# Weight halves, deferred transposes and background modulation in a hybrid diffusion layer

## The chip, the cores and the metric

The kernel runs on one core of a Trainium2 chip. The metric is device time in microseconds for one execution; where several executions were timed, the median is given. TensorE multiplies, VectorE and ScalarE do elementwise work, GpSimd does some sums and memsets and issues some DMAs, and the sync engine issues most DMAs. Each of these takes its own instructions in a fixed order.

## What is computed

One layer of a diffusion backbone, in float32, for 256 latent tokens and 256 context tokens of width 2048:

```python
mod_x = split(silu(c) @ w_mod + b_mod, 6)           # shift1, scale1, gate1, shift2, scale2, gate2
mod_c = split(silu(c_ctx) @ w_mod + b_mod, 6)
h  = rms_norm(x, g_mix) * (1 + mod_x[1]) + mod_x[0]   # the same for ctx with mod_c
qa, ka, va, qb, kb, vb, rb, lrf, lrb, gate_a, gate_b = split(h @ w_in)
o_attn = windowed_attention(qa, ka, va, context keys and values, sink)
o_gla  = bidirectional_gated_linear_attention(qb, kb, vb, decays from lrf, lrb)
y = (sigmoid(gate_a) * (o_attn @ w_attn_o)
     + sigmoid(gate_b) * ((rms_norm(o_gla) * silu(rb)) @ w_gla_o)) @ w_out
x = x + mod_x[2] * y
u = depthwise_conv3((rms_norm(x, g_ffn) * (1 + mod_x[4]) + mod_x[3]) @ w_up)
out = x + mod_x[5] * ((silu(u[:, :5632]) * u[:, 5632:]) @ w_down)
```

The weights are some 400 MB of float32, and each is used once.

## The kernel before

**Products in halves.** A float32 operand is split into a high half `hi` (rounded to the matmul type by ScalarE, line 61) and a low half `lo = x - hi` (VectorE, line 62). A product is three matmuls: hi·hi, hi·lo and lo·hi. `wload` (137) loads a chunk of 256 rows by 512 columns, 512 KB, into a ring of four buffers `raw`, on the sync engine's queue; `wsplit` (143) makes its halves `whi` and `wlo` in rings of three buffers each, at high priority.

**Projections.** `proj_nat` (152) computes tokens by features. Per chunk and per tile of 128 tokens it runs, for each of the two row tiles, activation-high by weight-high, activation-high by weight-low, activation-low by weight-high (163 to 165): 12 matmuls of 512 columns a chunk for two token tiles, 24 for four. `proj_T` (169) computes features by tokens, the weights stationary and 256 tokens moving: 24 matmuls a chunk (186 to 189), 48 when the context is taken along. Both accumulate in the four PSUM banks of the pool `acc`; at the end `evac` empties them.

**Ticks.** Before each chunk, `tick` (124) hands out work that runs beside the projections: `beside`, a generator with a pace (gated linear attention, or attention), and `bg_steps`, a list of steps with the pace `bg_rate`.

**Background modulation.** shift1 and scale1 are needed first, for both token kinds, and are computed on TensorE by `mod_both`. The other four parts, for the latent tokens alone, are done by `mod_latent` (225): for each part and each of four groups of 512 columns, eight steps, each of which loads 256 rows with `wload`, into the same `raw` ring and on the same queue as the weights, and adds them to `macc` with two VectorE instructions of 512 elements (line 239). After the last step of a group come a 32x32 transpose, a reduction, a tiny matmul on TensorE (247) and copies into the column tiles.

**Stages.** The order of the program is: shift1 and scale1 with the first projections (to about 220 us), gated linear attention for four heads beside the projections of its keys and values (to about 485), attention keys and values (to about 600), four query blocks with the attention of the block before beside them (to about 800), the GLA output gate, the merge of both branches and the output projection (to about 1300), and the ConvFFN in two halves, each with up-projections and then down-projections. The pace of the background is 0.7 steps a chunk in the first of these with background, then 2.0 for keys and values, 0 beside the attention, 0.5 until the output projection, where what remains is done at once.

**Transposes.** Attention keys (`ka_evac`, 676) and queries (`qa_block`, 689) are normalised and rotated by `norm_rope` on VectorE and ScalarE and transposed on TensorE in the evacuation itself. So are the gated GLA output and the merged branches (`to_T`, 776), and the residual stream (`wo_evac`, 838).

A scheduler orders each engine's instructions when the program is built, by priority and by what it expects to be ready; on the chip each engine then keeps that order. `W2(tag, ...)` takes a tile from a ring whose number of buffers stands in `F2_BUFS`; `bank` takes a PSUM bank, one for `main`, three for `side`.

Of the kernel before, what the change touches and what calls it, by code (L numbers as in the profile page):

```python
# [16 lines left out]
P = 128  # L17
# [13 lines left out]
def layer_kernel(ctx, tc, A, out):  # L31
# [6 lines left out]
    wr = pool(name="wr", bufs=4)  # L38
    wh = pool(name="wh", bufs=3)
# [8 lines left out]
    F2_BUFS = {"fa": 4, "fb": 4, "fc": 6, "mod": 2}  # L48
# [17 lines left out]
    def load(dst, src):  # L66
        """a load by the sync engine; while chain is open, issued in the order of the program"""
# [34 lines left out]
    def columns(name, parts, eng=G):  # L102
        rows = W2("mod", "rows", [P, P])
# [18 lines left out]
    beside = []  # L122

    def tick():
        """the steps of `beside`, a generator and its pace, and of the list"""
# [26 lines left out]
    def proj_nat(w, r0, c0, kts, lhs, evac):  # L152
        """out[token, feature] for 512 features; lhs[tile](kt) -> (hi, lo) [K, 128]"""
        banks = [acc.tile([P, 512], F32, name="acc", tag="acc") for _ in lhs]
        for k0 in kts[::2]:
# [3 lines left out]
            for i, l in enumerate(lhs):  # L159
                for k in range(nk):  # L160
                    kt = k0 + k
                    ahi, alo = l(kt)
                    PE.matmul(banks[i], ahi, hi[:, k, :], start=(kt == kts[0]), stop=False)  # L163
                    PE.matmul(banks[i], ahi, lo[:, k, :], start=False, stop=False)  # L164
                    PE.matmul(banks[i], alo, hi[:, k, :], start=False, stop=(kt == kts[-1]))  # L165
# [3 lines left out]
    def proj_T(w, c0, kts, rhs, evac):  # L169
        """out[feature, token] for 512 features; rhs: list of f(kt) -> (hi, lo) [K, 256]"""  # L170
# [3 lines left out]
        for k0 in kts[::2]:  # L174
# [3 lines left out]
            for f in range(4):  # L178
                for k in range(nk):
                    kt = k0 + k  # L180
                    whi, wlo = (x[:, k, f * P:(f + 1) * P] for x in (hi, lo))
                    for i, r in enumerate(rhs):
                        b = (f % per) if n == 1 else i
                        o = banks[f // per][:, b * T:(b + 1) * T]
                        ahi, alo = r(kt)
                        PE.matmul(o, whi, ahi, start=(kt == kts[0] and b == 0), stop=False,  # L186
                                  skip_group_check=True)
                        PE.matmul(o, whi, alo, start=False, stop=False, skip_group_check=True)  # L188
                        PE.matmul(o, wlo, ahi, start=False, stop=(kt == kts[-1]), skip_group_check=True)  # L189
# [6 lines left out]
    def mod_both(part, t0, n, dst):  # L196
        """steps for c and c_ctx on the tensor engine; dst[p, c, kt] for kt = t0..t0+n-1"""
# [27 lines left out]
    def mod_latent(part, j, dst):  # L225
        """steps for c alone: products summed over the row tiles on the vector engine"""
        a = []
        c0 = part * D + j * 512

        def step(k0):  # L230
            if k0 == 0:
                a.append(W2("mod", "macc", [P, 512]))
            raw = wload(w_mod[k0 * P:k0 * P + 256, c0:c0 + 512])
            for k in range(2):
                kt = k0 + k
                if kt == 0:
                    V.tensor_scalar(a[0], raw[:, 0, :], ccol[:, 0:1], None, op0=ALU.mult)
                else:
                    V.scalar_tensor_tensor(a[0], raw[:, k, :], ccol[:, kt:kt + 1], a[0],  # L239
                                           op0=ALU.mult, op1=ALU.add)  # L240
            if k0 == KT - 2:
                tr = W2("mod", "mtr", [P, 16, 32])
                V.transpose(tr.rearrange("p a c -> p (a c)"), a[0])
                rs = sm.tile([P, 16], F32, name="mrs", tag="mrs", bufs=2)
                V.tensor_reduce(rs, tr, op=ALU.add, axis=AX.X)
                pc = bank("pcl", (32, 16))
                PE.matmul(pc, sel[:, 0:32], rs, start=True, stop=True)
                pv = pc.rearrange("p (a b) -> p b a", b=4)
                d = dst[:, 4 * j:4 * j + 4]
                for b4 in range(4):  # L250
                    V.tensor_copy(d[32 * b4:32 * b4 + 32, :], pv[:, b4, :])
                b0 = part * 16 + j * 4
                V.tensor_tensor(d, d, bmod[:, b0:b0 + 4], op=ALU.add)

        return [lambda k0=k0: step(k0) for k0 in range(0, KT, 2)]
# [20 lines left out]
    def rms_scale(ss, n, shape):  # L276
        """(ss / n + eps) ** -0.5: exp(-ln / 2) with a Newton step"""
# [12 lines left out]
    def token_rows(tag, name, cols):  # L290
        """one factor a token, [P, 1] per tile of tokens, as a row in every partition"""
# [666 lines left out]
```

## Time and profile before

| what | value |
|---|---|
| runs | 2060.81, 2062.3 and 2058.01 us; median 2060.81 |
| profiled execution | span 2061.8 us from its first instruction to its last |
| mean granted TensorE clock | 0.990 of full speed |
| DMA | 413.71 MB, mean 201 GB/s |
| transfers on the sync queue | 406.89 MB |
| transfers on the GpSimd queue | 4.74 MB |

The page's chain of waits puts 60% of the span on TensorE, 11% on DMA, 8% on VectorE and 2% on ScalarE, with 18% of time in which an engine waited for nothing that the profile shows. In a row of a group, the numbers after the bar are the busy time, the mean duration of one instruction in ns, and the idle time of the engine just before the group's instructions with what ended it. A matmul's duration includes the depth of the pipeline, so that matmuls overlap, and their pace is read from counts in a stretch. A row of a stretch has its bounds, its length, and for each engine the busy time and the number of instructions, in the order TensorE, its weight loads, VectorE, ScalarE, GpSimd, and then the granted clock, the DMA share and GB/s. A row of waits has who waited for whom, the sum in us, how many times, and the longest.

### The profile page before, as it was taken

How to read it: one execution, taken by the hardware profiler on the slowest of the kernel's cores; microseconds unless marked ns; L12 is line 12 of the kernel's file. 1: busy time of each engine (PE TensorE's matmuls, PEld its weight loads, DVE VectorE, ACT ScalarE, POOL GpSimd, SP SyncE). 2: the span in 40 equal slices, each digit the busy share in tenths (PEclk: the TensorE clock that was granted, in tenths of full speed). 3: DMA queues.
4: the chain of work that ended last, by engine and by line, in shares of the span. 5: the costliest groups of instructions: out<-in, count | busy, mean ns of one | idle time of the engine just before them, and what ended most of it. 6: DMA issues, size and time to landing. Idle time of an engine off the chain costs nothing.

```text
span 2061.8 us, 30115 instructions
## 1 busy us (share of the span) xinstructions
PE 1999.2 (97%) x11792; PEld 1721.8 (84%) x11792; DVE 1405.7 (68%) x2149; ACT 937.4 (45%) x1306; POOL 41.9 (2%) x62
## 2 busy tenths in 40 slices
PE   6899999999999999999999999899999999999999
PEld 4679888888787777777787788899999889999987
DVE  4666778978867888777767665666666555666654
ACT  3323464552346665443334344554455334445533
POOL 0001100001000000000000000000000000000000
PEclk8999999999999999999999999999999999999999
DMA  9976434347664466787888875566666566666664
GB/s 347 337 247 197 120 111 123 113 118 226 213 186 114 121 194 192 254 270 260 264 279 272 294 235 184 164 184 184 184 183 184 194 193 187 184 184 183 183 209 150
DMA packets 214350, 413.71 MB, mean 201 GB/s; under 512 B 12548, under 2 KB 21092, under 8 KB 213184
## 3 DMA queue, kind: packets, MB, share of 16 engines
q1 hardware_dynamic: 212320, 406.89, 63.3%
q0 software_dynamic: 1360, 4.74, 0.8%
q8 instruction: 92, 1.51, 0.3%
q14 instruction: 50, 0.41, 0.1%
q10 hardware_dynamic: 528, 0.17, 0.0%
HBM read 409.63 MB, written 2.11 MB: 200 GB/s over the span
## 4 chain that ended last, share of the span: by engine, by line
PE 60%; issue 18%; DMA 11%; DVE 8%; ACT 2%; POOL 0%; DVEq 0%; ACTq 0%; POOLq 0%
PE acc L189 10%; PE acc L186 10%; PE acc L188 10%; PE acc L165 8%; PE acc L164 8%; PE acc L163 8%; DMA raw<-in_w_mod 8%; DVE wlo L62 3%; DVE macc L239 2%; DMA raw<-in_w_in 2%; PE pm L210 1%; PE pa L503 1%; ACT whi L61 1%; DMA raw<-in_w_gla_o 1%; PE po L589 1%
## 5 line engine op out<-in xcount | busy, mean ns | idle before, releaser
L61 ACT ACTIVATE whi<-raw 128x1024 fp32r<-128x1024 f32 x568 | 601.4, 1059 | 863.7 <-PE acc L165 366.4
L62 DVE TENSOR_TENSOR wlo<-raw,whi 128x1024 fp32r<-128x1024 f32 x568 | 693.3, 1222 | 428.3 <-ACT whi L61 422.7
L186 PE MATMUL acc<-h2h,whi 128*128 128x256 f32 x1408 | 399.5, 284 | 1.3 <-ACT h2h L346 1.3
L188 PE MATMUL acc<-h2l,whi 128*128 128x256 f32 x1408 | 399.5, 284 | 0.0
L189 PE MATMUL acc<-h2h,wlo 128*128 128x256 f32 x1408 | 399.2, 284 | 0.0
L186 PEld LDWEIGHTS acc<-h2h,whi 128*128 128x128 f32 x1408 | 271.3, 193 | 1.9 <-ACT h2h L346 1.8
L188 PEld LDWEIGHTS acc<-h2l,whi 128*128 128x128 f32 x1408 | 271.3, 193 | 0.2
L189 PEld LDWEIGHTS acc<-h2h,wlo 128*128 128x128 f32 x1408 | 271.3, 193 | 0.0
L239 DVE SCALAR_TENSOR_TENSOR macc<-raw,ccol,macc 128x512 f32<-128x512 f32 x240 | 180.6, 752 | 100.5 <-DMA raw<-in_w_mod 97.2
L163 PE MATMUL acc<-whi,h01hi 128*128 128x512 f32 x352 | 139.5, 396 | 0.9 <-ACT whi L61 0.9
L164 PE MATMUL acc<-wlo,h01hi 128*128 128x512 f32 x352 | 139.1, 395 | 1.3 <-DVE wlo L62 1.2
L163 PE MATMUL acc<-whi,h00hi 128*128 128x512 f32 x352 | 139.2, 395 | 0.0
L164 PE MATMUL acc<-wlo,h00hi 128*128 128x512 f32 x352 | 139.0, 395 | 0.2 <-DVE wlo L62 0.2
L165 PE MATMUL acc<-whi,h00lo 128*128 128x512 f32 x352 | 138.6, 394 | 0.0
L165 PE MATMUL acc<-whi,h01lo 128*128 128x512 f32 x352 | 138.2, 392 | 0.0
L163 PE MATMUL acc<-whi,ah 128*128 128x512 f32 x352 | 137.0, 389 | 0.0
L164 PE MATMUL acc<-wlo,ah 128*128 128x512 f32 x352 | 137.0, 389 | 0.0
L165 PE MATMUL acc<-whi,al 128*128 128x512 f32 x352 | 136.9, 389 | 0.0
L164 PEld LDWEIGHTS acc<-wlo,h01hi 128*128 128x128 f32 x352 | 66.4, 189 | 16.0 <-DVE wlo L62 3.2
L163 PEld LDWEIGHTS acc<-whi,h01hi 128*128 128x128 f32 x352 | 66.4, 189 | 14.3 <-ACT whi L61 1.3
L164 PEld LDWEIGHTS acc<-wlo,h00hi 128*128 128x128 f32 x352 | 66.2, 188 | 14.1 <-DVE wlo L62 1.3
L165 PEld LDWEIGHTS acc<-whi,al 128*128 128x128 f32 x352 | 66.1, 188 | 13.8
(369 smaller groups left out, 3393.2 us busy)
## 6 DMA issues: line engine op xcount, KB each, us to landing
raw<-in_w_in SPq DMA_DIRECT2D x208, 512.0 KB, 4.2
raw<-in_w_up SPq DMA_DIRECT2D x176, 512.0 KB, 3.7
raw<-in_w_mod SPq DMA_DIRECT2D x128, 512.0 KB, 3.9
raw<-in_w_down SPq DMA_DIRECT2D x88, 512.0 KB, 3.8
mraw<-in_w_mod SPq DMA_DIRECT2D x32, 1024.0 KB, 10.2
raw<-in_w_attn_o SPq DMA_DIRECT2D x32, 512.0 KB, 4.8
raw<-in_w_gla_o SPq DMA_DIRECT2D x32, 512.0 KB, 5.2
raw<-in_w_out SPq DMA_DIRECT2D x32, 512.0 KB, 3.8
```

The source lines that it names most:

```text
L61: S.activation(hi, src, AF.Copy)
L62: V.tensor_tensor(lo, src, hi.bitcast(F32), op=ALU.subtract)
L163: PE.matmul(banks[i], ahi, hi[:, k, :], start=(kt == kts[0]), stop=False)
L164: PE.matmul(banks[i], ahi, lo[:, k, :], start=False, stop=False)
L165: PE.matmul(banks[i], alo, hi[:, k, :], start=False, stop=(kt == kts[-1]))
L186: PE.matmul(o, whi, ahi, start=(kt == kts[0] and b == 0), stop=False, skip_group_check=True)
L188: PE.matmul(o, whi, alo, start=False, stop=False, skip_group_check=True)
L189: PE.matmul(o, wlo, ahi, start=False, stop=(kt == kts[-1]), skip_group_check=True)
L210: PE.matmul(a[0][q:q + 32, :], cS[:, kt, :], raw[:, k, :], start=(kt < 4), stop=(kt >= 12))
L239: V.scalar_tensor_tensor(a[0], raw[:, k, :], ccol[:, kt:kt + 1], a[0], op0=ALU.mult, op1=ALU.add)
L503: PE.matmul(pa[:, t, :], k2[:, dt, t * P:(t + 1) * P], q2[:, dt, tq * P:(tq + 1) * P], start=(dt == 0), stop=(dt == 1))
L589: PE.matmul(po, x_, y_[:, s, :], start=(n == 0), stop=(n == 11))
```

## The change

- The ring `raw` has three buffers instead of four, `whi` and `wlo` four each instead of three.
- `proj_nat` and `proj_T` run all products of a chunk with the weight's high half first, for all tiles, and then all with its low half.
- `defer(n, fn)` puts a function on a list; `tick` runs it n + 1 ticks later, before the other work of that tick, and `flush` runs all. The transposes in `ka_evac`, `qa_block`, `to_T` (both uses) and `wo_evac` are deferred by it.
- `mod_latent` takes several parts and goes in steps of 128 rows by 1024 columns, 512 KB, with one VectorE instruction of 1024 elements a step. Its loads have a ring of two buffers of their own and go on GpSimd's queue, each issued two steps ahead of its use; the first two wait for a given tile (`behind`): the first GLA keys, or for the last part the FFN's norm factors. The tiny matmuls are deferred by three ticks.
- The last part, gate2, moves from before the output projection to the first up-projections. Its row in every partition (`gate2`) is made before the first down-projections instead of at the FFN's start.
- Paces: the background 0.3 (was 0.7), 1.6 (was 2.0), 0.52 (was 0.5), and 0.36 in the FFN; the attention 1.4 from -2.9 (was 0.8 from 0).
- For space, the tiles `rows` share a ring with other small tiles, `mtr` goes to `fb`, and the scratch for GpSimd's DMA descriptors is 4096 bytes a partition.

```diff
-    wr = pool(name="wr", bufs=4)
-    wh = pool(name="wh", bufs=3)
+    wr = pool(name="wr", bufs=3)
+    wh = pool(name="wh", bufs=4)
...
-    F2_BUFS = {"fa": 4, "fb": 4, "fc": 6, "mod": 2}
+    F2_BUFS = {"fa": 4, "fb": 4, "fc": 6, "macc": 1, "mraw": 2}
...
+    later = []
+    def defer(n, fn):
+        later.append([n, fn])
+    def flush():
+        while later:
+            later.pop(0)[1]()
     def tick():
+        for e in later:
+            e[0] -= 1
+        while later and later[0][0] < 0:
+            later.pop(0)[1]()
...
                     PE.matmul(banks[i], ahi, hi[:, k, :], start=(kt == kts[0]), stop=False)
-                    PE.matmul(banks[i], ahi, lo[:, k, :], start=False, stop=False)
-                    PE.matmul(banks[i], alo, hi[:, k, :], start=False, stop=(kt == kts[-1]))
+                    PE.matmul(banks[i], alo, hi[:, k, :], start=False, stop=False)
+            for i, l in enumerate(lhs):
+                for k in range(nk):
+                    kt = k0 + k
+                    PE.matmul(banks[i], l(kt)[0], lo[:, k, :], start=False, stop=(kt == kts[-1]))
...
+    def mod_latent(parts, behind):
+        seq = [(part, dst, j, kt) for part, dst in parts for j in range(2) for kt in range(KT)]
+        raws, a = {}, [None]
+        def get(i):
+            if i < len(seq):
+                part, _, j, kt = seq[i]
+                c0 = part * D + j * 1024
+                raws[i] = W2("mraw", "mraw2", [P, 1024])
+                if i < 2:
+                    V.tensor_copy(raws[i][:, 0:1], behind)
+                G.dma_start(raws[i], w_mod[kt * P:(kt + 1) * P, c0:c0 + 1024])
...
+        def step(i):
+            part, dst, j, kt = seq[i]
+            if i == 0:
+                get(0)
+                get(1)
+            raw = raws.pop(i)
+            if kt == 0:
+                a[0] = W2("macc", "macc", [P, 1024])
+                V.tensor_scalar(a[0], raw, ccol[:, 0:1], None, op0=ALU.mult)
+            else:
+                V.scalar_tensor_tensor(a[0], raw, ccol[:, kt:kt + 1], a[0], op0=ALU.mult, op1=ALU.add)
+            get(i + 2)
+            if kt == KT - 1:
+                finish(part, dst, j)
...
-    for part, dst in ((3, shift2), (4, scale2), (2, gcol1), (5, gcol2)):
-        for j in range(4):
-            bg_steps.extend(mod_latent(part, j, dst))
-    bg_rate[:] = [0.7, 0.0]
+    bg_steps.extend(mod_latent(((3, shift2), (4, scale2), (2, gcol1)), kbt[:, 3, 0:1]))
+    bg_rate[:] = [0.3, 0.0]
...
-        pt = bank("ptk", (P, 4, P))
-        for h in range(4):
-            PE.transpose(pt[:, h, :], z[:, h, :], ident)
-        split(kTh[:, :, i * P:(i + 1) * P], kTl[:, :, i * P:(i + 1) * P], pt)
-    bg_rate[0] = 2.0
+        def turn():
+            pt = bank("ptk", (P, 4, P))
+            for h in range(4):
+                PE.transpose(pt[:, h, :], z[:, h, :], ident)
+            split(kTh[:, :, i * P:(i + 1) * P], kTl[:, :, i * P:(i + 1) * P], pt)
+        defer(1 + i // 2, turn)
+    bg_rate[0] = 1.6
...
-        beside[:] = [attend(g, qTs), 0.8, 0.0]
+        beside[:] = [attend(g, qTs), 1.4, -2.9]
...
-    bg_rate[0] = 0.5
+    bg_rate[0] = 0.52
...
-            to_T(s_, gh, gl, j, t)
+            defer(1 + t, lambda: to_T(s_, gh, gl, j, t))
...
-    while bg_steps:
-        bg_steps.pop(0)()
...
+    flush()
     s1 = sm.tile([P, 2], F32, name="s1", bufs=1)
...
-    gate2 = rows_from_cols("gate2", gcol2)
+    bg_steps.extend(mod_latent([(5, gcol2)], r1[:, 0:1]))
+    bg_rate[:] = [0.36, 0.0]
...
+        if half == 0:
+            flush()
+            gate2 = rows_from_cols("gate2", gcol2)
```

`proj_T` is changed in the same way as `proj_nat`; the query and residual transposes are wrapped in a `turn` like the key ones, with `defer(2 + t, turn)` and `defer(1 + t, turn)`.

More of the change, by code (lines that the diff above doesn't have):

```diff
@@ L102, in columns @@
     def columns(name, parts, eng=G):
-        rows = W2("mod", "rows", [P, P])
+        rows = sm.tile([P, P], F32, name="rows", tag="t128", bufs=2)
         n = 0
@@ L223, in mod_both, with finish @@
         return [lambda k0=k0: step(k0) for k0 in range(0, KT, nk)]
[L225 to L243, printed above, removed]
+    def mod_latent(parts, behind):
[9 more added lines that the diff above has]
+                G.dma_start(raws[i], w_mod[kt * P:(kt + 1) * P, c0:c0 + 1024])
+        def finish(part, dst, j):
+            for q in range(2):
+                tr = W2("fb", "mtr", [P, 16, 32])
+                V.transpose(tr.rearrange("p a c -> p (a c)"), a[0][:, q * 512:(q + 1) * 512])
@@ L253, in step, with out @@
-                V.tensor_tensor(d, d, bmod[:, b0:b0 + 4], op=ALU.add)
-        return [lambda k0=k0: step(k0) for k0 in range(0, KT, 2)]
+                c = 8 * j + 4 * q
+                def out(rs=rs, c=c):
+                    pc = bank("pcl", (32, 16))
+                    PE.matmul(pc, sel[:, 0:32], rs, start=True, stop=True)
+                    pv = pc.rearrange("p (a b) -> p b a", b=4)
+                    d = dst[:, c:c + 4]
+                    for b4 in range(4):
+                        V.tensor_copy(d[32 * b4:32 * b4 + 32, :], pv[:, b4, :])
+                    V.tensor_tensor(d, d, bmod[:, part * 16 + c:part * 16 + c + 4], op=ALU.add)
@@ L257, in rows_from_cols @@
+        return [lambda i=i: step(i) for i in range(len(seq))]
     def rows_from_cols(name, col):
@@ L693, in evac, with turn @@
             z = norm_rope(b, rq, t)
[L694 to L697 removed]
+            def turn():
+                pt = bank("ptq", (P, 4, P))
+                for h in range(4):
+                    PE.transpose(pt[:, h, :], z[:, h, :], ident)
+                split(qT[:, 0, :, t * P:(t + 1) * P], qT[:, 1, :, t * P:(t + 1) * P], pt)
+            defer(2 + t, turn)
         proj_nat(w_in, 0, QA + g * 512, ALL, h_x, evac)
```

58 lines of the change are left out of this document (27 added, 31 removed).

## The prediction

> **What bounds the kernel now.** I read the page's busy shares first, then equal and unequal stretches of the span, then who waits for whom in the stretch with the most idle TensorE time.
>
> ```profile
> span 2061.8 us, 30115 instructions
> PE 1999.2 (97%) x11792; PEld 1721.8 (84%) x11792; DVE 1405.7 (68%) x2149; ACT 937.4 (45%) x1306; POOL 41.9 (2%) x62
> ...
> 1400.00:1500.00 100.00, 100.00 (x836) 100.00 (x835) 63.17 (x81) 50.91 (x63) 0.00 (x0) 1.00 0.64 183
> 1600.00:1700.00 100.00, 100.00 (x443) 82.80 (x442) 51.63 (x50) 39.26 (x37) 0.00 (x0) 1.00 0.60 192
> ...
> 200.00:480.00 280.00, 274.52 (x1656) 236.47 (x1656) 225.47 (x422) 148.44 (x293) 23.90 (x29) 1.00 0.41 120
> 480.00:600.00 120.00, 115.64 (x509) 94.10 (x508) 88.16 (x150) 36.38 (x52) 5.68 (x9) 0.97 0.71 216
> 600.00:800.00 200.00, 199.15 (x932) 156.32 (x932) 168.84 (x351) 119.27 (x212) 0.58 (x1) 1.00 0.53 155
> 800.00:1200.00 400.00, 384.12 (x1688) 307.77 (x1687) 297.23 (x379) 164.03 (x172) 0.00 (x0) 1.00 0.81 266
> 1320.00:1580.00 260.00, 260.00 (x2169) 260.00 (x2169) 163.10 (x210) 132.00 (x163) 0.00 (x0) 1.00 0.64 184
> ```
>
> TensorE bounds it, and two rows give its undisturbed pace: 100 us / 836 = 0.120 us for a 256-wide product (up-projection, 1400 to 1500) and 100 / 443 = 0.226 us for a 512-wide one (down-projection, 1600 to 1700). The change adds no product and takes none of these away, so all it can win is time in which TensorE falls behind that pace. From 1320 to the end there is none to win. The last columns of each row are the granted clock (1.00 nearly everywhere, 0.97 from 480 to 600), the share of DMA time and GB/s.
>
> From 800 to 1200 (GLA output and merge) TensorE is short of the pace by the most:
>
> ```profile
> 800.00:1200.00 400.00, 9.18 (x56) 6.20 (x56) 1.00 0.81 266
> ...
> PE pto L779 <- DVE m L820: 5.0, 3, 2.2
> PE acc L164 <- DVE wlo L62: 5.0, 9, 2.0
> PE pto L779 <- DVE sr L789: 3.1, 3, 1.9
> ...
> PEld acc L164 <- DVE wlo L62: 11.4, 17, 2.4
> PEld pto L779 <- DVE m L820: 7.3, 6, 2.6
> ...
> DVE macc L239 <- DMA raw<-in_w_mod: 67.9, 44, 3.4
> ...
> SPq L68 <- DVE wlo L62: 201.3, 134, 4.4
> SPq L68 <- DVE macc L239: 73.1, 65, 2.1
> SPq L68 <- DMA raw<-in_w_mod: 33.5, 30, 2.9
> ```
>
> The first row is line 779 alone in that stretch: 56 transposes, 9.2 us. The other 1688 - 56 instructions at 0.226 us are 368.8 us, together 378, so 22 us of 400 are lost. The rows below name the losers: TensorE meets a low half that VectorE has not yet made (L164), and transposes whose source is still in VectorE's queue (L779). Behind both stands the third group: VectorE, which works in order, sat 67.9 us waiting for modulation loads, and every low half queued behind such a wait is late. The sync queue, also in order, waited 73.1 + 33.5 us on buffers that hold modulation data, with weight loads behind them: weights and modulation share one ring of four.
>
> **The change, part by part.** *Low halves last.* A chunk of 12 products now begins with 8 that need only the high half: 8 x 0.226 = 1.8 us in which the low half may still come. It covers most of a wait whose longest is 2.0 us on TensorE. The same count of products and of weight loads remains, and in the undisturbed stretch all three kinds cost alike, so the order itself costs nothing:
>
> ```profile
> L186 PE MATMUL acc<-h2h,whi 128*128 128x256 f32 x1408 | 399.5, 284 | 1.3 <-ACT h2h L346 1.3
> L188 PE MATMUL acc<-h2l,whi 128*128 128x256 f32 x1408 | 399.5, 284 | 0.0
> L189 PE MATMUL acc<-h2h,wlo 128*128 128x256 f32 x1408 | 399.2, 284 | 0.0
> ```
>
> *Transposes deferred.* The 8.1 us of L779 waits go if the source is ready one or two chunks (2.8 to 5.5 us) later; the longest wait was 2.2 us on TensorE, so it is. In the key projection one wait stands alone:
>
> ```profile
> PE ptk L680 <- DVE sq L671: 4.4, 1, 4.4
> ...
> PE pa L568 <- DVE kf L561: 3.2, 4, 1.0
> PE pa L503 <- DVE q L523: 2.3, 4, 0.9
> ```
>
> It goes with the deferral, and with it some of the 3% of clock missing from 480 to 600, but four tiles must be normalised there before their turn; I take 4 us, from a bound of 0 to 8 (4.4, and 3% of 120 us). The two GLA rows (5.5 us) are not deferred; VectorE merely has less beside them (pace 0.3 instead of 0.7), so I take 3.
>
> *Modulation in 1024-wide steps, own ring, GpSimd's queue.* The work on VectorE, and the loads:
>
> ```profile
> L61 ACT ACTIVATE whi<-raw 128x1024 fp32r<-128x1024 f32 x568 | 601.4, 1059 | 863.7 <-PE acc L165 366.4
> ...
> L62 DVE TENSOR_TENSOR wlo<-raw,whi 128x1024 fp32r<-128x1024 f32 x134 | 162.8, 1220 | 30.0 <-ACT whi L61 29.4
> L239 DVE SCALAR_TENSOR_TENSOR macc<-raw,ccol,macc 128x512 f32<-128x512 f32 x122 | 91.4, 750 | 69.5 <-DMA raw<-in_w_mod 67.9
> ...
> L820 DVE TENSOR_TENSOR m<-m,m 128x512 f32<-128x512 f32 x6 | 4.1, 682 | 0.0
> ...
> raw<-in_w_in SPq DMA_DIRECT2D x68, 512.0 KB, 4.6
> raw<-in_w_mod SPq DMA_DIRECT2D x64, 512.0 KB, 4.0
> raw<-in_w_attn_o SPq DMA_DIRECT2D x32, 512.0 KB, 4.8
> raw<-in_w_gla_o SPq DMA_DIRECT2D x32, 512.0 KB, 5.2
> ...
> raw<-in_w_up SPq DMA_DIRECT2D x89, 512.0 KB, 3.7
> ...
> att<-in_k_amask POOLq DMA_DIRECT2D x1, 512.0 KB, 3.8
> ...
> 433.77 0.58 POOL L638 DMA_DIRECT2D att<-in_k_amask  x1
> ```
>
> Going from 512 to 1024 elements adds 1220 - 682 = 538 ns to a two-operand instruction, so a step is an estimated 750 + 538 = 1.29 us against 2 x 0.75. Steps by the paces in the diff: 32 chunks x 0.3 and 16 x 1.6 make 35 before the attention, and the other 61 of 96 follow at 0.52 a chunk, 0.52 x 2.80 us. (2.80 is 378 us over the 134 weight chunks that the L62 row counts.) So a step comes each 5.4 us there, and its load is issued two steps, 10.8 us, ahead. It needs 0.58 us of issue and 3.8 to 5.2 us of transfer: 4 us to spare, so VectorE's 67.9 us of waiting should go, and its own work on these steps falls from 91 us to 61 x 1.29 = 79. GpSimd's queue holds a load until the step two before is done; the memsets, sums and loads queued behind it wait for at most one VectorE step. With the sync queue free of these loads, a weight load goes out when its own buffer comes free.
>
> Of the 22 us lost from 800 to 1200 I take 20 as won.
>
> *Three raw buffers instead of four.* This is the cost. The weight ring now turns three times in 8.4 us (3 x 2.80). One turn is a landing of 4.6 to 5.2 us, the high half (1.06, the L61 row), the low half (1.22), and at worst one modulation step in front of it (1.29): 6.9 to 8.8. Before, 196 loads (the four rows of that stretch) passed four buffers in 400 us, 4 x 400 / 196 = 8.2 us a turn at most. So it fits on average, and a fourth pair of halves lies between it and TensorE. Priced from 0 to 134 x (8.8 / 3 - 2.80) = 18 us; nearer 0 because the step stands in front only sometimes. I take 0 beyond the 2 us left above.
>
> *The FFN gets the gate's modulation.* 32 steps at 0.36 a chunk of 24 x 0.120 = 2.88 us, one each 8 us: VectorE rises from 163 / 260 = 63% by 16 points, and DMA from 184 by 0.52 MB / 8 us = 66 to 250 GB/s, less than the 266 borne above. A turn is 3.7 to 5.2 + 1.06 + 1.22 + 0 to 1.29 = 6.0 to 8.8 against 8.6: between 0 and 96 chunks x 0.05 = 5 us, taken as 1. What leaves is the second gate's transpose and row at the FFN's start, taken as 2 us won with the waits around it:
>
> ```profile
> 1300.00:1320.00 20.00, 14.62 (x92) 13.59 (x93) 14.78 (x35) 11.15 (x25) 1.06 (x2) 0.74 0.42 131
> ```
>
> *Start and attention.* To about 100 us DMA bounds the kernel; raw plus split buffers stay seven, so it should neither gain nor lose, bound -4 to +4. In the attention (600 to 800) only 0.85 us of TensorE is idle; the steps start later and come denser (1.4 a chunk), VectorE is already 84% busy, so 0, with a bound of +8.
>
> **Sum**: -20 - 4 - 3 + 1 - 2 = -28 us on a span of 2061.8 us is 2034. The page shows nothing around the span; the median of the runs, 2060.8, lies 1 us below it, so I forecast 2033, with 2020 to 2045 from the bounds taken together.
>
> **A rule against the change.** The amask row is a GpSimd load of the same 512 KB, issued in a stretch (200 to 480) where VectorE was busy 225 of 280 us, and it landed in 3.8 us, as sync's do. The Trainium skill, "SBUF — State Buffer", section "SBUF: two separate sides", says that VectorE instructions in a two-port mode lock GpSimd out of writing its descriptors, so its DMAs start late. If GpSimd could write only in VectorE's idle quarter (1 - 297 / 400), 0.58 us would become 2.3. In the key and value projections, with a step each 5.4 / 1.6 = 3.4 us from two buffers, the turn would be 2.3 + 4.3 + 1.29 = 7.9 instead of 6.8, so 26 steps lose 0.55 each, 14 us, and the sum would be 2047. I go by the row and give the lock-out 2 in 100.
>
> **Rivals.** *All of it goes.* Every wait named above vanishes, with the upper bounds of the others: 22 + 8 + 5.5 + 3 (FFN's start) + 4 (start) = 42 us, 2018. For it: four split buffers and halves late by under 2 us. Against: sources on one in-order VectorE that stays 74% busy.
>
> *The waits move.* Deferred transposes and attention steps meet their sources late again, since the order on TensorE is fixed beforehand and VectorE's queue is not shorter at those points; half the gain stays: 2047. For it: the four normalised key tiles need VectorE together with 1.6 steps a chunk.
>
> *The three-buffer ring becomes the bound: slower.* If the GpSimd transfers slow the weight loads to 6.5 us (14 loads from 140 to 200 took a median of 6.0), a turn is 6.5 + 1.06 + 1.22 + 1.29 = 10.1 us, 3.36 a chunk. From 800 to 1200 that is 134 x 3.36 = 450 instead of 400, and the first up-projections lose 96 x (3.36 - 2.88) = 46; with the 9 us won elsewhere 2148. At 5.8 us it is 3.12: +18 + 23 - 9, or 2093. It decides from a turn of 3 x 400 / 134 = 9.0 us on. For it: the ring loses a quarter while the bytes stay. Against: at most 8.2 us a turn now, including the head-of-line waits that go.
>
> ```profile
> raw<-in_w_in SPq DMA_DIRECT2D x14, 512.0 KB, 6.0
> ```
>
> *Nothing to be had*: the idle time is a byproduct of the pace and only shifts into the FFN, 2060.
>
> **How the numbers follow.** Forecast 52%; all of it 12%; waits move 15%; lock-out 2%; ring bound 15%; nothing 4%. The likeliest gives 2033. Below 2014 and above 2056 about 18% is left out, nearly all of it the ring; the first four share 2014 to 2050. A measurement of this kernel tells about 0.2% (4 us) from no change. Faster: the first four, 81%; same 4%; slower 15%.
>
> **What would show it.** Right: from 800 to 1200 some 1780 matmuls instead of 1688; no VectorE wait on modulation loads above a few us; no L680 wait; sync's waits only on low halves; the FFN still at 836 a 100 us. Wrong: high halves waiting for weight DMAs by more than 100 us from 800 to 1200, weight landings of 6 us and more, TensorE below 100% in the first up-projections, or VectorE waiting for GpSimd's loads.

## The result, and the profile after

The change made the kernel slower, by 0.9%. After: 2080.1 us, median of 4 runs (2077.0 to 2085.2). Before, timed beside it: 2061.6 us, median of 4 (2058.0 to 2064.5). The ratio is 1.0093, with a 95% interval of 1.0075 to 1.0111. The forecast was 2033 us within 2014 to 2056.

The page of the kernel after, its span and busy shares:

```profile
span 2079.6 us, 30019 instructions
PE 2002.6 (96%) x11792; PEld 1728.8 (83%) x11792; DVE 1382.6 (66%) x2025; ACT 932.1 (45%) x1306; POOL 106.1 (5%) x190
```

VectorE has less to do than before (1382.6 against 1405.7 us), as forecast, and TensorE has the same 11792 products; yet the span is 18 us longer. Unequal stretches of it (length, then busy time and instructions of TensorE, its weight loads, VectorE, ScalarE and GpSimd, granted clock, DMA share, GB/s) say where:

```profile
200.00:480.00 280.00, 267.94 (x1592) 228.66 (x1592) 202.68 (x364) 145.63 (x289) 31.16 (x44) 0.99 0.34 102
480.00:600.00 120.00, 114.17 (x497) 92.21 (x496) 87.64 (x129) 35.12 (x53) 19.42 (x42) 0.97 0.67 212
800.00:1200.00 400.00, 390.15 (x1728) 316.93 (x1727) 271.08 (x303) 169.60 (x182) 24.99 (x47) 0.98 0.75 244
1320.00:1580.00 260.00, 250.31 (x2061) 249.33 (x2061) 196.16 (x252) 124.09 (x155) 15.91 (x30) 0.98 0.74 234
...
900.00:1000.00 100.00, 92.54 (x389) 73.92 (x388) 81.87 (x86) 38.28 (x39) 13.81 (x26) 0.93 0.89 307
1000.00:1200.00 200.00, 199.95 (x893) 164.61 (x892) 103.03 (x112) 85.88 (x88) 0.00 (x0) 1.00 0.65 205
```

From 200 to 480 TensorE is busy for 267.94 us instead of 274.52. From 800 to 1200 it got 1728 products done instead of 1688, not the 1780 of the forecast. The FFN's up-projections (1320 to 1580), where nothing was to be won, lost 10 us. The last two rows take the stretch apart: from 900 to 1000 TensorE is idle for 7.5 us in 100 at a clock of 0.93, and from 1000 on it is at its full pace. GpSimd's column shows the difference: it issues modulation loads in the one (26 instructions) and none in the other.

The same in time, from the two traces: when TensorE began its n-th product of a projection (us).

```
product    before    after   after - before
   400      125.2    119.5    -5.7
   800      193.5    188.2    -5.3
  1600      375.1    378.3    +3.1
  2800      742.9    752.6    +9.7
  3600      961.9    978.4   +16.5
  4800     1253.4   1256.0    +2.6
  6000     1431.5   1434.3    +2.8
  6400     1479.5   1495.7   +16.2
 10271     2056.6   2073.7   +17.0
```

After loses 22 us between products 800 and 3600, where its first 96 modulation steps run, and wins 14 back from 3600 to 4800, where its steps are done and those of before are not. From 4800 to 6000, with 24 of the FFN's 32 steps, it loses next to nothing; then 13 us go at one place, between 6000 and 6400. The waits of the kernel after, TensorE's and then VectorE's (who waits for whom: us in total, times, longest; the last row is VectorE's from 800 to 1200 alone):

```profile
PE pcl L267 <- DVE gcol L271: 6.8, 1, 6.8
...
PE pcl L267 <- DVE scale L271: 3.2, 2, 2.8
...
PE pcl L267 <- DVE shift L271: 2.3, 1, 2.3
...
DVE macc L286 <- DMA mraw<-in_w_mod: 76.1, 69, 3.5
...
DVE macc L286 <- DMA mraw<-in_w_mod: 22.2, 27, 2.3
```

VectorE still stands 76.1 us on modulation loads, against 97.2 in the whole span before. From 800 to 1200 the wait fell from 67.9 to 22.2 us; but 26.0 us now stand from 480 to 620 (9.3 before) and 20.2 in the FFN, where there were none. New is `pcl`, the tiny products that fold a finished 1024-wide sum: there are now two in a row, they share the one bank of the kind `main`, and TensorE, in order, stands at the second until VectorE has copied the first one out. VectorE's timeline around the longest of these waits (start, length, instruction, what ended the idle time before it):

```profile
1460.68 1.28 DVE L286 SCALAR_TENSOR_TENSOR macc<-mraw,ccol,macc 128x1024 f32<-128x1024 f32 x1 [1.84 <-DMA mraw<-in_w_mod]
...
1463.02 0.14 DVE L271 COPY gcol<-pcl 32x4 f32<-32x4 f32 x1
...
1465.78 1.20 DVE L62 TENSOR_TENSOR wlo<-raw,whi 128x1024 fp32r<-128x1024 f32 x1
...
1470.92 0.49 DVE L271 COPY gcol<-pcl 32x4 f32<-32x4 f32 x3
```

The first of the four copies runs at 1463.02, the other three at 1470.92; between them stand 7.8 us of other work in VectorE's fixed order. TensorE is idle, and then slow:

```profile
1466.00:1472.00 6.00, 0.45 (x3) 0.45 (x4) 5.91 (x12) 3.87 (x6) 0.00 (x0) 0.54 0.74 225
1472.00:1476.00 4.00, 4.00 (x20) 4.00 (x21) 2.46 (x8) 1.06 (x1) 0.00 (x0) 0.50 0.61 201
```

After the wait the granted clock is 0.50 (20 products in 4 us, 33 at the pace of 0.120 us). By the timeline the slow pace lasts to 1476.8: 23 products in 5.0 us instead of 2.8. So 7.0 us of waiting cost about 9.3; three shorter waits before it (1.8, 0.4 and 1.2 us) make up most of the rest of the 13 us lost there. The Trainium skill, "TensorE: Matmul & The Clock Gate", "Part 1: The HAM clock gate (the "warmup" mystery)", says that the gate knows only half and full rate; the 0.50 agrees.

The steps themselves, VectorE's groups from 830 to 990 us (busy time and mean ns, then idle time before them):

```profile
L62 DVE TENSOR_TENSOR wlo<-raw,whi 128x1024 fp32r<-128x1024 f32 x50 | 60.9, 1217 | 4.0 <-ACT whi L61 3.7
L286 DVE SCALAR_TENSOR_TENSOR macc<-mraw,ccol,macc 128x1024 f32<-128x1024 f32 x44 | 56.5, 1283 | 21.9 <-DMA mraw<-in_w_mod 21.7
...
L284 DVE TENSOR_SCALAR macc<-mraw,ccol 128x1024 f32<-128x1024 f32 x3 | 2.2, 748 | 0.0
```

A step was to come about every second chunk (0.52 a chunk, 5.4 us). Here are 44 and 3 (L284 is the first of each sum) for 50 chunks, 160 / 47 = 3.4 us apart, and they hold VectorE for 56.5 + 21.9 + 2.2 = 81 of 160 us. In the FFN all 32 came from 1328 to 1478 us, one each 4.7 us instead of 8. The pace in the program is not the place in VectorE's queue: the order of each engine is fixed when the program is built, and it has the steps early. Counted by low halves on VectorE, against the version that holds each step at its place (e5), the first 96 steps of after stand 21 chunks early on average. Those of before stand only one chunk early, against the same remedy there (e9), and keep their rate: 27 steps for 54 chunks in the same 160 us.

Modulation steps ahead of their pace is theory B below. Its rivals: A, the shared bank of the tiny products; C, three raw buffers instead of four; D, the low-halves-last order moves waits instead of covering them.

### The profile page after: what moved, and what is told of

It is laid out like the page before. It is cut to its first block, busy times and chain, and to the rows that moved or that the text cites. A ratio compares the mean times of both kernels' runs of the same rounds, so it can differ in the third digit from the quotient of the medians.

```text
span 2079.6 us, 30019 instructions
## 1 busy us (share of the span) xinstructions
PE 2002.6 (96%) x11792; PEld 1728.8 (83%) x11792; DVE 1382.6 (66%) x2025; ACT 932.1 (45%) x1306; POOL 106.1 (5%) x190
## 3 DMA queue, kind: packets, MB, share of 16 engines
q0 software_dynamic: 19792, 71.85, 10.8%
## 4 chain that ended last, share of the span: by engine, by line
PE 61%; issue 18%; DMA 12%; DVE 7%; ACT 2%; SPq 0%; POOL 0%; DVEq 0%; ACTq 0%; POOLq 0%
PE acc L203 14%; PE acc L176 11%; PE acc L181 11%; PE acc L177 11%; DMA mraw<-in_w_mod 8%; PE acc L206 7%; DVE wlo L62 2%; DVE macc L286 2%; DMA raw<-in_w_up 2%; PE pa L539 1%; DMA raw<-in_w_in 1%; PE po L625 1%; PE pm L227 1%; PE pa L604 1%; ACT whi L61 1%
## 5 line engine op out<-in xcount | busy, mean ns | idle before, releaser
L203 PE MATMUL acc<-h2h,whi 128*128 128x256 f32 x1408 | 348.2, 285 | 1.5 <-ACT h2h L382 1.5
L206 PE MATMUL acc<-h2l,whi 128*128 128x256 f32 x1408 | 348.2, 285 | 0.0
L286 DVE SCALAR_TENSOR_TENSOR macc<-mraw,ccol,macc 128x1024 f32<-128x1024 f32 x120 | 154.4, 1287 | 76.7 <-DMA mraw<-in_w_mod 76.1
L203 PE MATMUL acc<-h2h,wlo 128*128 128x256 f32 x1408 | 199.6, 285 | 2.9 <-DVE wlo L62 1.8
L203 PEld LDWEIGHTS acc<-h2h,wlo 128*128 128x128 f32 x1408 | 183.1, 194 | 3.5 <-DVE wlo L62 2.2
L181 PE MATMUL acc<-wlo,h00hi 128*128 128x512 f32 x352 | 100.0, 399 | 0.8 <-DVE wlo L62 0.8
L181 PE MATMUL acc<-wlo,h01hi 128*128 128x512 f32 x352 | 97.4, 393 | 0.0
L255 POOL DMA_DIRECT2D mraw<-in_w_mod x128 | 68.1, 533 | 564.2 <-DVE macc L286 324.4
L181 PE MATMUL acc<-wlo,ah 128*128 128x512 f32 x352 | 94.1, 389 | 0.0
L176 PEld LDWEIGHTS acc<-whi,h00hi 128*128 128x128 f32 x352 | 67.3, 191 | 18.1 <-DVE val L62 3.3
```

The source lines that it names most:

```text
L181: PE.matmul(banks[i], l(kt)[0], lo[:, k, :], start=False, stop=(kt == kts[-1]))
L203: PE.matmul(o, w_, ahi, start=(kt == kts[0] and b == 0 and part == 0), stop=(kt == kts[-1] and part == 1), skip_group_check=True)
L206: PE.matmul(o, w_, alo, start=False, stop=False, skip_group_check=True)
L255: G.dma_start(raws[i], w_mod[kt * P:(kt + 1) * P, c0:c0 + 1024])
L286: V.scalar_tensor_tensor(a[0], raw, ccol[:, kt:kt + 1], a[0], op0=ALU.mult, op1=ALU.add)
```

## The experiments

Times are medians of 4 to 10 runs; the ratio is to the kernel before, timed beside each; "paced" means each step held at its place (e5).

```
                                us      ratio, 95% interval
after                         2080.1   1.0093 (1.0075 to 1.0111)
e1  after, one bank           2066.5   1.0025 (1.0009 to 1.0040)
e2  after, loads late         2193.3   1.0644 (1.0618 to 1.0670)
e3  after, raw 4 / halves 3   2067.5   1.0030 (1.0015 to 1.0046)
e4  before, lo last           2076.4   1.0073 (1.0052 to 1.0094)
e5  after, paced              2039.9   0.9891 (0.9877 to 0.9906)
e6  e1 and e3 together        2060.8   0.9990 (0.9974 to 1.0006)
e7  after, old order          2069.4   1.0039 (1.0025 to 1.0052)
e8  before, deferral          2062.7   1.0007 (0.9996 to 1.0018)
e9  before, paced             2048.3   0.9937 (0.9918 to 0.9955)
e10 paced, old order          2034.9   0.9866 (0.9850 to 0.9882)
e11 paced, one bank           2035.6   0.9870 (0.9855 to 0.9885)
e12 paced, raw 4 / halves 3   2040.7   0.9898 (0.9882 to 0.9915)
e13 e10 with one bank         2030.0   0.9852 (0.9837 to 0.9866)
e14 e10, no transpose deferred 2035.3  0.9874 (0.9858 to 0.9891)
e15 after, FFN's steps paced  2067.1   1.0032 (1.0021 to 1.0043)
```

**e1: both tiny products in one bank.**

```diff
-                    pc = bank("pcl", (32, 16))
-                    PE.matmul(pc, sel[:, 0:32], rs, start=True, stop=True)
+                pc = bank("pcl", (32, 32))
+                for q in range(2):
+                    PE.matmul(pc[:, 16 * q:16 * q + 16], sel[:, 0:32], rss[q], start=True, stop=True)
```

> The kernel after, with one edit: the two tiny products that end a group of 1024 modulation columns go into one PSUM tile and are copied out together, so that the second no longer waits for VectorE to empty the only bank of its kind. Theory A (that wait is the loss): the waits beside these products, 2.4 us at 528, 3.4 at 583, 7.3 at 941 to 951 and 7.0 at 1464, go, with the half-clock stretches behind them; 2080 becomes 2055 to 2062. Theory B (VectorE is late because modulation steps run ahead of their pace and stand on loads): the lateness only shows at other waits, 2070 to 2080. Theory C (three raw buffers): 2076 to 2082.

2066.5 us, 14 less than after, between the ranges of A and B. The bank is part of the loss, not all: VectorE still stood 70.9 us on modulation loads. The Trainium skill, "Perfetto Trace Analysis", "Matmuls", asks that independent groups of products rotate through banks so that emptying one lies beside filling the next. The trace of after agrees as far as it goes: without a second bank its second product waits, 12.3 us in all. e1 does without rotation, since both products are emptied together; no run gave them a second bank.

**e2: each load waits for the low half of the chunk before,** by a one-element copy on GpSimd into the load's buffer.

```diff
                 if i < 2:
                     V.tensor_copy(raws[i][:, 0:1], behind)
+                else:
+                    G.tensor_copy(raws[i][:, 0:1], last_lo[0][:, 0, 0:1].bitcast(F32))
```

> The kernel after, with one edit: each modulation load from the third on waits for the low half of the weight chunk before it, through a one-element copy on GpSimd into its buffer, so that the steps can't run ahead of their pace. Theory B: steps spread from one each 3.1 us to one each 5 to 6 us between 830 and 1150, VectorE's waits for modulation loads fall from 76 us to under 30, the GLA stretch (230 to 360) gets 5 to 8 us back, and the total is 2055 to 2065. Theory A: the bank waits stay where both products are due together, with a VectorE that is less late: 2068 to 2078. Theory C: 2076 to 2082.

A miss, 2193.3 us. The steps did move back in VectorE's order, to 3 chunks ahead of e5's places on average instead of 21, but a load that waits for a low half of the weights isn't there yet when its step's turn comes. VectorE's wait for them and one that follows on TensorE:

```profile
DVE macc L291 <- DMA mraw<-in_w_mod: 266.5, 90, 7.0
...
PE acc L184 <- DVE wlo L62: 27.2, 13, 4.5
```

So the rate of the steps alone doesn't decide: with nearly the rate that B asks for, 190 us more of standing made the kernel 113 us slower than after. An instruction that stands in an in-order queue before its data is dear even when it is early by little.

**e3: four raw buffers, three pairs of halves,** as before the change.

```diff
-    wr = pool(name="wr", bufs=3)
-    wh = pool(name="wh", bufs=4)
+    wr = pool(name="wr", bufs=4)
+    wh = pool(name="wh", bufs=3)
```

> The kernel after with the rings of before: four raw buffers, three pairs of halves. Theory C: weight loads are issued earlier, ScalarE's waits for weight loads (146 us in the kernel after) halve, and the total is 2055 to 2066. Theories A and B: within 5 us of 2080.

2067.5 us, 13 less, nearest to C, and ScalarE's waits for weight loads halved as C had said (146 to 70 us). Yet the tiny products still stopped TensorE, and VectorE stood 77.2 us on its loads. e12 shows what this is worth.

**e4: the kernel before with the new order of products alone** (`proj_nat` and `proj_T` of after).

> The kernel before with one edit: the products with the low half come last in each chunk. If the order is worth what the prediction gave it, the waits on low halves (L164, 11.4 us between 800 and 1200) go: 2048 to 2056. If it only moves them, 2058 to 2064. If the order costs pace by itself, above 2064.

2076.4 us: slower by 14 than the kernel before, timed beside it (2062.3). TensorE's largest wait in this kernel, which was 5.0 us before:

```profile
PE pto L783 <- DVE m L824: 14.9, 3, 5.9
```

TensorE's waits on low halves from 800 to 1200 went (5.0 to 0.4 us), and the merge's transposes behind them wait instead. From 200 to 480 its busy time falls too, from 274.52 to 269.17 us. D holds: the order moves the wait.

**e5: the steps held at their pace.** Each step's VectorE instruction is ordered behind the low half of the chunk before its tick; nothing else differs from after.

```diff
-                V.tensor_scalar(a[0], raw, ccol[:, 0:1], None, op0=ALU.mult)
+                with tc.issue_after(last_lo[0].ins):
+                    V.tensor_scalar(a[0], raw, ccol[:, 0:1], None, op0=ALU.mult)
             else:
-                V.scalar_tensor_tensor(a[0], raw, ccol[:, kt:kt + 1], a[0], op0=ALU.mult, op1=ALU.add)
+                with tc.issue_after(last_lo[0].ins):
+                    V.scalar_tensor_tensor(a[0], raw, ccol[:, kt:kt + 1], a[0], op0=ALU.mult, op1=ALU.add)
```

> After, but each modulation step's VectorE instruction is put, in VectorE's order, behind the low half of the chunk before the point where the step is due; loads are issued as in after. Theory B (steps that run ahead of their pace make VectorE stand on modulation loads, 76.1 us, and that costs most of the loss): VectorE's wait for these loads falls below 20 us, the steps from 800 to 1200 come about every 5 us, and the time is 2052 to 2068 us. Theory A (the one shared bank of the two tiny products) alone: the two tiny products still stop TensorE for 5 us or more somewhere, and the time stays at 2074 to 2086 us. Theory C (three raw buffers): ScalarE's waits for weight loads stay near 90 us in the input products, time 2072 to 2084 us.

2039.9 us: 40 less than after, more than B had asked for, and neither A's nor C's range holds it. Its stretches, VectorE's wait for modulation loads from 800 to 1200, and its groups from 830 to 990:

```profile
480.00:600.00 120.00, 119.62 (x535) 96.98 (x534) 76.50 (x119) 39.49 (x58) 14.45 (x31) 1.00 0.63 191
...
800.00:1200.00 400.00, 398.86 (x1795) 327.62 (x1794) 280.64 (x308) 173.29 (x182) 27.00 (x51) 1.00 0.80 257
...
1320.00:1580.00 260.00, 259.92 (x2089) 255.89 (x2088) 196.05 (x256) 127.33 (x158) 14.27 (x27) 1.00 0.76 237
...
DVE macc L290 <- DMA mraw<-in_w_mod: 2.1, 2, 1.3
...
L62 DVE TENSOR_TENSOR wlo<-raw,whi 128x1024 fp32r<-128x1024 f32 x58 | 70.9, 1222 | 32.0 <-ACT whi L61 31.6
L290 DVE SCALAR_TENSOR_TENSOR macc<-mraw,ccol,macc 128x1024 f32<-128x1024 f32 x30 | 38.4, 1279 | 2.1 <-DMA mraw<-in_w_mod 2.1
...
L287 DVE TENSOR_SCALAR macc<-mraw,ccol 128x1024 f32<-128x1024 f32 x2 | 1.5, 748 | 0.0
```

30 and 2 steps for 58 chunks, 160 / 32 = 5.0 us apart, close to the 5.4 that the prediction had reckoned; 2.1 us of standing; 1795 products from 800 to 1200, where 1780 had been forecast. VectorE now idles before its low halves because it waits for ScalarE (31.6 us): it is ahead of its inputs. The waits at the tiny products went as well (0.4 us left from 800 to 1200), with the bank unchanged.

**e6: e1 and e3 together.**

> After, with both tiny products in one bank and with four raw buffers and three pairs of halves. If A (-14 us alone) and C (-13 us alone) are two losses that add, 2080 - 27 = 2053, within 2049 to 2058 us. If both remove the same stall (VectorE late at the tiny products), the time stays at 2062 to 2068 us.

2060.8 us, between the two ranges, over runs from 2052.9 to 2065.8; whether A and C add is not settled by it. Both together only reach the time of the kernel before.

**e7: after with the old order of products.**

> After, with the products of a chunk in the order of before (each k: high by high, high by low half, low by high). Theory D (the order itself moves waits from the low halves to the transposes, as alone in the kernel before, +14 us): 2064 to 2074 us. The prediction's view (the order covers late low halves, and the deferral covers the transposes): slower than after, 2084 to 2100 us, with TensorE waiting for low halves by 10 us or more from 800 to 1200.

2069.4 us: D again, 11 us less than after. From 800 to 1200 the waits on low halves come back (5.2 us instead of 0.8), as the prediction's view had it, but those at the transposes go.

**e8: the kernel before with the deferral of the transposes** and the attention's new pace alone.

> Before, with the deferral of the transposes and the attention's new pace (1.4, begun 2.9 late) alone. The prediction's view: the transposes' waits go (8.1 us from 800 to 1200, 4.4 at the key projection), 2046 to 2056 us. If deferral only shifts the wait to another instruction of the fixed order: 2058 to 2066 us. If it delays what needs the transposed tiles: over 2066 us.

2062.7 us: no difference that can be told. TensorE's waits at these transposes shrank to 1.5 us, and low halves came late instead (in the whole span 9.1 us at this line, 5.0 before):

```profile
PE acc L175 <- DVE wlo L62: 9.1, 13, 1.8
...
PE pto L798 <- DVE m L839: 1.5, 2, 0.8
...
DVE macc L250 <- DMA raw<-in_w_mod: 103.0, 69, 3.9
```

**e9: the kernel before with its steps held at their pace,** nothing else of the change.

> Before, with nothing of the change, but each modulation step's VectorE instructions put behind the low half of the chunk before the point where the step is due. If VectorE standing on modulation loads (67.9 us from 800 to 1200) was what cost the kernel before its 22 us, and the place of the steps is the whole remedy: 2035 to 2048 us. If the own ring is needed with it (a modulation load that is read later holds one of the four shared raw buffers longer, and weight loads come late): 2058 to 2085 us, with ScalarE's waits for weight loads above 150 us in all.

2048.3 us: 13 less than before, at the edge of the first range, for a move of one chunk. From 800 to 1200 VectorE's wait on these loads fell from 67.9 to 3.2 us:

```profile
DVE macc L243 <- DMA raw<-in_w_mod: 3.2, 2, 1.6
```

ScalarE waited 115.6 + 34.5 + 27.9 = 178 us for weight loads. That is over the second theory's 150, but it was 171 in before as well: holding the steps back in the shared ring made it little worse and took none of it away. In e5 these three waits are under 60 us.

**e10, e11, e12: one part each on top of e5:** the old order of products, one bank, four raw buffers.

> The kernel with the steps in their pace (2039.9 us), with the products in the old order. The prediction's view (the order covers low halves that are late): 2046 to 2060 us, TensorE waiting for low halves by 5 us or more from 800 to 1200. Theory D (the order moves waits and is a loss by itself, as in the kernel before, +14, and in after, +11): 2026 to 2034 us. If the order only mattered while VectorE was late: 2037 to 2043 us.

> The kernel with the steps in their pace (2039.9 us), with both tiny products in one bank. If the shared bank costs by itself (theory A as a cause of its own): 2026 to 2034 us. If it cost only because VectorE was late at the copies: no change, 2036 to 2044 us.

> The kernel with the steps in their pace (2039.9 us), with four raw buffers and three pairs of halves. Theory C (three raw buffers are a loss by themselves): 2026 to 2034 us. If three raw buffers hurt only while steps came in bursts on VectorE: 2036 to 2046 us.

e12 has 2040.7 us: three raw buffers cost nothing once the steps come in pace, so e3's 13 us were a consequence of the bursts, and C falls as a cause of its own. ScalarE's waits for the input weights say the same: 90.2 us in after, 48.3 with four buffers (e3), 46.7 with three and the steps paced (e5). e10 (2034.9) and e11 (2035.6) lie 4 to 5 us below e5, just above the ranges of D and A, and the interval of each overlaps that of e5.

**e13: the old order and one bank, paced.**

> The steps in their pace, the products in the old order and both tiny products in one bank. Alone beside the paced steps (2039.9 us) the old order gave -5 and the one bank -4. If both gains are real and separate: 2029 to 2033 us. If they take the same microseconds or were chance: 2033.5 to 2038 us.

2030.0 us, the lowest of all; its interval lies clear of e5's, so together the two are a gain of about 10. Its stretch from 800 to 1200:

```profile
800.00:1200.00 400.00, 400.00 (x1800) 329.93 (x1799) 278.17 (x284) 172.47 (x181) 27.52 (x52) 1.00 0.80 263
```

TensorE is busy for all 400 us, and the view of its waits lists none there. This version beats both kernels: 1.5% below before, 2.4% below after.

**e14: e10 without the deferral of the transposes.**

> The steps in their pace and the products in the old order (2034.9 us), with no transpose deferred (only the latent sums' small products still are). The prediction gave the deferral some 12 us (8.1 us of waits from 800 to 1200 and 4 at the key projection): 2043 to 2050 us. If the transposes' sources are in time once VectorE does not stand on loads: 2033 to 2040 us.

2035.3 against 2034.9 us: the deferral is worth nothing that can be told. One wait at a deferred transpose's place came back from 800 to 1200, of 1.3 us.

**e15: after with only the FFN's 32 steps paced.**

```diff
+                with (tc.issue_after(last_lo[0].ins) if part == 5 else contextlib.nullcontext()):
```

> After (2080.1 us), with the FFN's 32 modulation steps alone put behind the low half of the chunk before the point where they are due; the 96 steps before keep their places. If a step that runs ahead costs where it stands (the trace of after falls 12.6 us behind the paced kernel inside the FFN, at 1464 us): 2064 to 2071 us, with TensorE at 100% from 1320 to 1580. If the loss sits in the 96 earlier steps and the FFN's stall follows from them, or if the shared bank stops TensorE there all the same: 2075 to 2084 us.

2067.1 us. The whole gain lies in the FFN (in the two traces 12.6 us between products 5600 and 6400), and TensorE is busy there again:

```profile
1320.00:1580.00 260.00, 259.92 (x2165) 259.24 (x2164) 203.40 (x267) 129.25 (x161) 15.85 (x30) 1.00 0.77 243
```

So of the 40 us between after and e5, 13 belong to the FFN's steps and the rest, 27, to the 96 before them. e1 took away a part of the same stall from the other side: between products 6000 and 6400 it gains 7 of its 14 us, so its gain and e15's overlap there; the two together were not run.

## Why the prediction was wrong

**The step that failed** is "So a step comes each 5.4 us there, and its load is issued two steps, 10.8 us, ahead", with "4 us to spare, so VectorE's 67.9 us of waiting should go". The rate of the ticks was taken for the order of VectorE's queue. (378 / 134 is 2.82, not the 2.80 written there; nothing hangs on it.) With loads of their own the steps ran nearly as fast as a ring of two lets them: 1.29 us of a step, 0.53 of issue and 4.4 of landing make 6.2 us for two, 3.1 each, and 3.4 was seen (4.7 in the FFN). At that rate nothing is to spare: VectorE went on standing on loads, with low halves and copies queued behind it and TensorE waiting for those. Holding the steps in their place, and nothing else, gives 2039.9 us: within the likeliest case's own range of 2020 to 2045, though two of the means that the sum relied on, the order and the deferral, have no part in it (e10, e14). What e5 changes is the standing, the early use of VectorE's time (from 830 to 990 the steps hold it for 81 of 160 us in after, 42 in e5), and when the loads go out; the weight loads' landing in that stretch differs little (4.8, 5.5 and 4.9 us in after for its three kinds, 4.6, 4.5 and 5.0 in e5). e2 shows that standing is dear even with the places nearly right, and e9, where a move of one chunk took it away, agrees. Early steps that never stand weren't tried, so the shares stay open.

**What the sum left out**: the tiny products. Two of them share one bank, and their copies lie scattered in VectorE's order: 12.3 us of TensorE's waits (6.8, 3.2 and 2.3), and the half clock behind the longest. Before, with one product at a time, TensorE never waited there for a copy (and 1.2 us for the sum itself). The wait needs a late VectorE (with e5 it is gone), so it is a second effect of the same step.

**Point by point.**
- *Low halves last, "covers most of a wait"*: wrong. +14 us alone in before (e4), and 11 us come back when it is undone in after (e7). What it won was 5 us at the start (product 400, in e4 as in after). The order cannot make VectorE's next result earlier; it lets TensorE meet the next one late.
- *Transposes deferred, 8.1 and 4 us*: wrong as a cause. 0 in before (e8) and 0 in the paced kernel (e14). The key projection did come right when paced: 119.62 us busy of 120 and a clock of 1.00 instead of 115.64 and 0.97, 4 us, but by VectorE's pace: e9 and e14, paced without the deferral, have 118.77 and 118.61 and a clock of 1.00, and e8, with the deferral alone, 115.77 and 0.97.
- *The GLA rows, 3 us to be won*: lost instead, and by the order of products, to which the sum gave no cost. These two waits grew from 5.5 to 8.4 us; in after with the old order (e7) they are 4.0, and TensorE is busy for 272.85 us of 280 instead of 267.94.
- *22 us lost from 800 to 1200, 20 to be won*: the size was right, and e13 wins all of it; the means were the pace and what e9 still lacks, not the order.
- *A step at 1.29 us*: 1.287 on average. *Three raw buffers at 0*: right once paced (e12); in after 13 us, through the bursts.
- *FFN +1*: 0 when paced, +13 in after, in the one stall before 1477. The steps' VectorE time fitted; their place did not. *FFN's start, 2 us to be won*: 0 (82.2 us before and 82.5 after between products 4800 and 5200).
- *The rivals.* "The waits move" was the nearest in kind, but with half the gain kept; its place was seen (the order fixed beforehand), its price not. The ring as the bound did not happen, though one sign of it, TensorE below 100% in the first up-projections, did: over the span weight loads landed as before, e15 has TensorE at its pace there with three buffers, and from 800 to 1200 high halves waited 33.8 us for input weights and 12.1 for the GLA output's, not 100. The lock-out of GpSimd, for which the Trainium skill, "SBUF — State Buffer", "SBUF: two separate sides", had been weighed, shows nowhere: the issue took 0.53 us and the landing 4.4 us with VectorE 66% busy.

The issue rows of the kernel after (KB each, median us to landing) and GpSimd's group for these loads:

```profile
raw<-in_w_in SPq DMA_DIRECT2D x208, 512.0 KB, 3.8
raw<-in_w_up SPq DMA_DIRECT2D x176, 512.0 KB, 3.8
mraw<-in_w_mod POOLq DMA_DIRECT2D x128, 512.0 KB, 4.4
...
raw<-in_w_attn_o SPq DMA_DIRECT2D x32, 512.0 KB, 4.2
raw<-in_w_gla_o SPq DMA_DIRECT2D x32, 512.0 KB, 4.5
...
L255 POOL DMA_DIRECT2D mraw<-in_w_mod x128 | 68.1, 533 | 564.2 <-DVE macc L286 324.4 <-DVE mraw L254 128.2 <-DVE macc L284 54.1
```

GpSimd spent its idle time waiting for buffers that VectorE held, not the other way about: the loads went out as soon as the early steps let them.

**Where the gain of the paced version lies.** Before to e9, the pace alone, 13 us; e9 to e14 another 13 for what is left beside order and deferral (own buffers on GpSimd's queue, wide steps, the gate's part in the FFN, the attention's pace), not split further, so no run shows what the own ring and queue are worth alone; by the two traces of e9 and e10, which show the same 13, 5 of them come between 742 and 858 us and 7 between 1138 and 1237 us, where e9 still has the gate's modulation to do. One bank and the old order bring it to e13.

## What to carry to other kernels

Background work that is issued "so many steps a chunk" has that pace only in the program's text; count in the trace how many steps stand between two chunks on the engine that runs them, and if they stand early, tie each to the instruction that it should follow. An own ring and queue for its loads lets such steps run ahead: in the shared ring they had stood one chunk early, with their own 21 (that the ring held them back is inferred; it wasn't tried alone). This change cost 18 us without the tie, and won 22 with it (e5). Before two small products go one after the other into one bank, look who empties it and what stands in that engine's queue between the copies.

## What the runs showed that was not expected

One rule of order moved more than any buffer: 40 us for e5 against 13 to 14 for a bank or a ring. Steps that stood a single chunk early cost the kernel before 13 us (e9). One wait of TensorE of 7.0 us cost about 9.3, since the clock stayed at half rate for 5 us behind it. And remedies for separate causes each gave 11 to 14 us in after (e1, e3, e7, e15), though with the steps paced the same edits (e11, e12, e10) gave 0 to 5: where an in-order engine is late, each change of its order shifts the lateness, and such gains are not evidence of separate causes.
